# Normalisation factors on GpSimd's queue, and pooled work placed behind the latest operand split

## The chip, the cores and the metric

The kernel runs on one core of one Trainium2 chip. The metric is the device time of one execution in microseconds (us). Engines are named as the profile names them: PE (TensorE), DVE (VectorE), ACT (ScalarE), POOL (GpSimd) and SP (SyncE). SP computes nothing; it issues DMAs.

## The reference

The reference is a trunk with one layer, a pooling mixer with a SiLU gate, between two RMS normalisations. The input `x` is 1 x 4096 x 1024 in float32. A mixer of a second kind stands in the file but isn't reached with one layer.

```python
def rms_norm(x, w):
    return x * lax.rsqrt(jnp.mean(x * x, axis=-1, keepdims=True) + 1e-6) * w

def pool_mixer(h, in_w, group_w, group_b, scale, out_w):
    u, gate = jnp.split(h @ in_w, 2, axis=-1)              # in_w: 1024 x 2048
    ug = u.reshape(b, s, 4, 256)
    pooled = jnp.stack([trailing_mean(ug[:, :, g], w)      # w = 2, 4, 8, 16 tokens
                        for g, w in enumerate((2, 4, 8, 16))], axis=2) - ug
    mixed = jnp.einsum('bsgc,gcd->bsgd', pooled, group_w) + group_b
    return (mixed.reshape(b, s, 1024) * scale * jax.nn.silu(gate)) @ out_w

def reference(x, norm_w, ...):
    h = x + pool_mixer(rms_norm(x, norm_w[0]), ...)
    return rms_norm(h, final_norm_w)
```

## The kernel before, in words

**Arithmetic.** Every float32 product is made of three matmuls. An operand is split into a rounded high part and the residual, its low part; the products high x high, high x low and low x high are added up in a bank of PSUM. `split` (the function at lines 153 to 156) makes both parts of a tile: ACT copies the source into the high part (the copy stands at line 151), then DVE subtracts that high part from the source and writes the low part (line 145). `latest_split[0]` holds the DVE instruction of the latest split.

**Products.** Each matrix product is cut into two by two blocks and done by a scheme of seven products, P1 to P7, in place of eight. Sums and differences of the blocks are formed on DVE (`add` at L142, `sub` at L145) before they are split, and the results are added up in PSUM and, in part, by DVE and ACT when banks are evicted.

**Steps.** The program is a list of steps, one product each. The 4096 tokens are four blocks b = 0 to 3 of 1024. First come 28 "a" steps, seven for each block (the first half of the channels and their gate), then 28 "b" steps, again seven for each block (the second half), all in the order P1, P2, P6, P7, P5, P4, P3, 48 matmuls each. Behind them stand 56 "o" steps, the output projection: eight blocks o0 to o7 of 512 tokens, in the order P1, P7, P6, P2, P5, P4, P3, 24 matmuls each. All of them are issued in `mm3` (L570).

**The main loop (L1171 to L1235).** For step n it records, in this order: loads for steps ahead; at "a" steps the factors of the next block (below); sums and differences for step n + 2 (`form`); the splits of a step ahead; pooled work that is due (`pool_due(n)`, L1210); the step itself (`run(n)`: its matmuls, then the evictions of its banks); at "a" steps a second call of `pool_due` (L1225). Each engine then works through its own instructions in the order in which they stand in its queue, and waits there where an instruction's inputs or its output buffer aren't ready. `tc.issue_after(instruction)` puts what is recorded inside it behind that instruction in the queue of an engine; it adds no work. All DMAs issued by SP stand in one queue too, with the waits in front of them.

**Evictions.** In "a" and "b" steps ACT copies P1's banks into other banks (L151, bank to bank), applies SiLU after P2, and copies or DVE adds (L142) the others. In "o" steps DVE adds the banks of most products onto the rows of `x` (L892).

**Pooled work.** `pool` (L617 to L669) takes the evicted tiles of one half of a block. For each of two channel groups it copies the last 16 columns of the half before into the tile's halo and saves its own last columns (ACT, tile `tails`), builds the trailing sums by one to four shifted additions (DVE, L142; for a window of two one subtraction, L145), scales them and subtracts the tile (DVE, L655), adds the bias and multiplies by the gate (DVE, L660, twice), and stores the result to DRAM (`yd`, SP, L664). It gives back the buffers (`vt`, `st`) at its end. `pool_later` (L974) notes the work after steps P4 and P3, due after a wait of some steps: 0 and 1 for "a"; 1 and 2 for "b", in the last block 2 and 5.

**Factors.** Each block's rows need a factor, 1 / sqrt(mean of squares + eps). For blocks 1 to 3 the factors come in two halves while the "a" steps of the block before run: rows of `x` are loaded (SP, L400), squared and summed (ACT, L407), the root is taken (ACT L192, DVE L196) and refined (POOL, L193 and L206 to L211). Then `store_rs` (L420) stores the half's 512 factors to DRAM, 2 KB, and `load_rstd` (L452) loads them back spread over all 128 partitions, 256 KB, once the store has landed. DVE multiplies the input tiles by them (L148) before they are formed and split. For block 0 the factors are spread by matmuls in `spread_rs`. Inputs for the coming steps (`xt`, L485) and the saved operands (`sd`) are loaded through SP as well; L476 saves operands through ACT's queue, a few of the first through GpSimd's.

**The last block.** During block 3's "b" steps the weights of the output projection (`wod`, loaded at L330) are brought in and split; the tiles `w` in the profile are theirs.

Of the kernel before, what the change touches and what calls it, by code (L numbers as in the profile page):

```python
# [15 lines left out]
P = 128  # L16
# [44 lines left out]
def kernel(  # L61
# [32 lines left out]
    nc = tc.nc  # L94
# [33 lines left out]
    def take(pattern="p (a b) -> p a b", pool=None, **sizes):  # L128
        sizes = sizes or {"a": 2}
        if pool is None:  # L130
            spare = len(vt.free) > keep[0] or not st.free
            pool = vt if spare and vt.age() < st.age() else st
        return pool.take(lambda t: t[:, 0:D].rearrange(pattern, **sizes))

    def take_v():
        return vt.take(lambda t: t.rearrange("p (a b) -> p a b", a=2))

    def give(ap):
        next(p for p in (st, vt, early, early5) if id(ap) in p.used).give(ap)

    def add(dst, a, b):
        nc.vector.tensor_tensor(out=dst, in0=a, in1=b, op=ALU.add)  # L142

    def sub(dst, a, b):
        return nc.vector.tensor_tensor(out=dst, in0=a, in1=b, op=ALU.subtract)  # L145

    def mul(dst, a, b):
        nc.vector.tensor_tensor(out=dst, in0=a, in1=b, op=ALU.mult)  # L148

    def copy(dst, src, func=AF.Copy):  # L150
        return nc.scalar.activation(dst, src, func)  # L151

    def split(dst, src):

        copy(dst[:, 0], src)
        latest_split[0] = sub(dst[:, 1], src, dst[:, 0].bitcast(F32)).ins

    latest_split = [None]

    colt = const.tile([P, 24], F32, name="colt")  # L160
    norm_c = [colt[:, k : k + 1] for k in range(NK)]
# [19 lines left out]
    rd = [[dram.tile([1, H], F32, name=f"rd{b}_{t}") for t in range(2)] for b in range(NB)]  # L181
# [125 lines left out]
    def split_wb(i):  # L307
        for h in range(2):
            (u,) = parts.pop((i, h)).values()
            if i == P1:  # L310
                split_scaled(w[i][h], u, pair(norm_c, h, 0))
            elif i == P2:
                split_scaled(w[i][h], u, pair(norm_c, h, 1))
            else:
                split(w[i][h], u)
            if i != P6:
                give(u)
# [9 lines left out]
    def load_w(src, i):  # L327
        for h in range(2):
            u = take()
            nc.sync.dma_start(out=u, in_=src[i][h])  # L330
            split(w[i][h], u)
            give(u)
# [25 lines left out]
    def split_early(place, u, pattern, **sizes):  # L358

        flat = place.rearrange("p s a b -> p s (a b)")  # L360
        split(flat, u.rearrange("p a b -> p (a b)" if len(u.shape) == 3 else "p k t c -> p (k t c)"))
        return [flat[:, j].rearrange(pattern, **sizes) for j in range(2)]
# [49 lines left out]
    def stats(b, half):  # L412
        ms = small.tile([P, 4], F32, tag="ms", name=f"ms{b}_{half}")
        tmp = small.tile([P, 4], F32, tag="tmp", name=f"tmp{b}_{half}")
        rs = small.tile([P, 4], F32, tag="rs", name=f"rs{b}_{half}")
        rsqrt(rs, tmp, ms, sums[b, half], b == 0)
        return rs

    def store_rs(b, half, rs):
        nc.sync.dma_start(out=rd[b][half][0].rearrange("(p j) -> p j", j=4), in_=rs)  # L420

    spread_done = [None]

# [23 lines left out]
    rstd = {}  # L447

    def load_rstd(b, half):
        if half == 0:  # L450
            rstd[b] = take()
        nc.sync.dma_start(out=rstd[b][:, half], in_=rd[b][half][0].partition_broadcast(P))  # L452

    def normalize(b, half, u):
        mul(u, u, rstd[b][:, half].unsqueeze(1).to_broadcast([P, 2, H]))
# [161 lines left out]
    def pool(b, q, half, vs, sgs):  # L617

        first = b == 0 and half == 1
        last = b == NB - 1 and half == 0  # L620
        end = HIST + H
        for g in range(2):
            grp = 2 * q + g
            win = 2 << grp
            v, sg = vs[g], sgs[g]
            if first:
                nc.vector.memset(v[:, :, 0:HIST], 0.0)
                if win == 2:
                    copy(v[:, :, HIST - 1 : HIST], v[:, :, HIST : HIST + 1])
            else:  # L630
                copy(v[:, :, 0:HIST], tails[:, g])
            if not last:
                copy(tails[:, g], v[:, :, H:])
            s = take_v()
            at = HIST
            if win == 2:
                sub(s[:, :, at:], v[:, :, at - 1 : end - 1], v[:, :, at:])
            else:
                lo = HIST - (win - 2)
                add(s[:, :, lo:], v[:, :, lo:end], v[:, :, lo - 1 : end - 1])  # L640
                n = 2
                while n < win:
                    lo = HIST - (win - 2 * n)
                    size = end - lo
                    a = at - HIST + lo
                    add(s[:, :, a - n : a - n + size], s[:, :, a : a + size],
                        s[:, :, a - n : a - n + size])
                    at -= n
                    n *= 2
                if first:  # L650
                    mul(
                        s[:, :, at : at + HIST], s[:, :, at : at + HIST],
                        invt[:, grp].unsqueeze(1).to_broadcast([P, 2, HIST]),
                    )
                nc.vector.scalar_tensor_tensor(  # L655
                    out=s[:, :, at : at + H], in0=s[:, :, at : at + H], scalar=1.0 / win,
                    in1=v[:, :, HIST:], op0=ALU.mult, op1=ALU.subtract,
                )
            for j in range(2):
                nc.vector.scalar_tensor_tensor(  # L660
                    out=sg[:, j], in0=s[:, j, at : at + H], scalar=bias_c[2 * grp + j],
                    in1=sg[:, j], op0=ALU.add, op1=ALU.mult,
                )
            nc.sync.dma_start(  # L664
                out=yd[2 * b + 1 - half][:, 2 * grp : 2 * grp + 2, :], in_=sg
            )
            give(v)
            give(s)
            give(sg)  # L669
# [302 lines left out]
    pending = []  # L972
# [11 lines left out]
        pending.append((n + wait, args))  # L984

    def pool_due(n):
        while pending and pending[0][0] <= n:
            pool(*pending.pop(0)[1])


    warm = nc.const_aps.tensor(1.0, [P, H], mybir.dt.bfloat16)
# [42 lines left out]
    with tc.high_priority():  # L1034
        rs = stats(0, 0)
# [43 lines left out]
    with tc.high_priority():  # L1079
        rs = stats(0, 1)  # L1080
# [90 lines left out]
    for n in range(2, len(steps)):  # L1171
        kind, b, i = steps[n]
# [3 lines left out]
        if ahead:  # L1176
            rows, squares = row_plan(b)
            for half, rs in scales.items():
                store_rs(b + 1, half, rs)
                load_rstd(b + 1, half)  # L1180
            scales.clear()
            for j in squares.get(i, ()):
                with tc.issue_after(evicted[0]):
                    square_row(b + 1, j // 4, j % 4)
                if j % 4 == 3:
                    scales[j // 4] = stats(b + 1, j // 4)
            for j in rows.get(i, ()):
                load_row(b + 1, j // 4, j % 4, early if b == 0 and i == P6 else None)
# [18 lines left out]
        if kind == "a" and b == 0:  # L1207
            with tc.issue_after(latest_split[0]):
                rest_of_first(n)
        pool_due(n)  # L1210
        since = n - (NB - 1) * len(ORDER_IN) - 2
        if 0 <= since < len(ORDER_IN):
# [9 lines left out]
        if kind in ("a", "b"):  # L1222
            pool_later(n)
            if kind == "a":
                pool_due(n)  # L1225
            if kind == "b" and b == NB - 1:
                load_w(wod, i)
            if kind == "b" and b in (1, 2) and i == P5:
                make_wo(b - 1)
            if kind == "b" and b == NB - 1 and i == P3:  # L1230
                f = take("p (a b) -> p a b", a=2)
                nc.sync.dma_start(
                    out=f.rearrange("p a b -> p (a b)"), in_=final_w.partition_broadcast(P)
                )
                fw.append(f)  # L1235
# [52 lines left out]
```

## Time and profile before

| | |
|---|---|
| median of 3 runs | 922.96 us (920.47 to 925.06) |
| profiled execution | 926.72 us |
| its span in the profile | 924.9 us, mean granted TensorE clock 0.995 |
| PE busy | 907.7 us, 98% of the span |
| DVE busy | 729.1 us, 79% |
| ACT busy | 449.4 us, 49% |
| POOL busy | 48.9 us, 5% |
| DMA | 177.01 MB, 191 GB/s in the mean |

Busy times are sums over an engine's instructions in one profiled execution. The span runs from the first to the last instruction of the profile; the device time of the same execution is 1.8 us longer. In rows of the timeline the first number is the start in us from the beginning of the span, the second the length; "x2" means that two alike instructions are told as one row, and brackets give the engine's idle time just before and what ended it. In rows of busy time by stretches, each engine's busy time is followed by its instructions in parentheses. Rows of waits give us in total, times, and the longest. Lines "L420" are lines of the kernel before.

### The profile page before, as it was taken

To read this page: it belongs to the slowest core of one execution; us is meant where nothing else is said; L and a number is where in the kernel's file an instruction comes from. 1 tells how busy PE (TensorE), PEld (TensorE's weight loads), DVE (VectorE), ACT (ScalarE), POOL (GpSimd) and SP (SyncE) were. 2 spreads that over 40 slices of the span, in tenths; PEclk is the share of its full clock that TensorE was granted. 3 is DMA by queue.
4 is the path that set the end of the run, shared out by engine and by line. 5 is a ranking of instruction groups with operands and counts; after the bars stand their busy time and mean duration, and the time that the engine had idled before them with its cause. 6 is when DMAs were issued, how large, how long until landed. Compare 5 with 4: busy or idle time off the path is not lost.

```text
span 924.9 us, 11163 instructions
## 1 busy us (share of the span) xinstructions
PE 907.7 (98%) x4212; PEld 791.0 (86%) x4212; DVE 729.1 (79%) x807; ACT 449.4 (49%) x685; POOL 48.9 (5%) x118
## 2 busy tenths in 40 slices
PE   9999989999999999999999999999999999999997
PEld 7888878888878888888888888888888888888886
DVE  3897992895698898597499399799997677677676
ACT  6868547347345655345343544653324424334333
POOL 0022100000000000000000000000201001001010
PEclk9999999999999999999999999999999999999999
DMA  9976766576756636115703563756567446365122
GB/s 344 402 305 202 276 227 173 182 258 229 251 225 226 210 113 228 46 46 187 290 23 122 198 227 114 259 155 199 188 224 233 137 176 228 112 207 199 51 92 91
DMA packets 67573, 177.01 MB, mean 191 GB/s; under 512 B 6720, under 2 KB 24512, under 8 KB 67520
## 3 DMA queue, kind: packets, MB, share of 16 engines
q1 hardware_dynamic: 61616, 156.37, 49.0%
q10 hardware_dynamic: 4176, 13.65, 3.8%
q0 software_dynamic: 1728, 6.29, 1.8%
q8 instruction: 33, 0.54, 0.2%
q14 instruction: 20, 0.16, 0.1%
HBM read 115.45 MB, written 60.83 MB: 191 GB/s over the span
## 4 chain that ended last, share of the span: by engine, by line
PE 58%; DVE 24%; DMA 10%; ACT 4%; issue 3%; POOL 1%; SPq 0%; DVEq 0%; ACTq 0%; POOLq 0%
PE bank L570 56%; DVE vt L142 6%; DVE op L145 5%; DVE st L145 3%; PE bank L373 2%; DVE st L148 2%; DVE vt L655 1%; DMA st<-in_out_w 1%; DMA rd<-rs 1%; DVE st L142 1%; DMA wod<-st 1%; DVE vt L660 1%; DMA st<-rd 1%; ACT op L151 1%; DMA st<-wvd 1%
## 5 line engine op out<-in xcount | busy, mean ns | idle before, releaser
L570 PE MATMUL bank<-op,w 128*128 128x512 f32 x2688 | 586.0, 381 | 8.4 <-DVE op L145 5.5
L570 PEld LDWEIGHTS bank<-op,w 128*128 128x128 f32 x2688 | 509.7, 190 | 83.9 <-DVE op L145 7.6
L570 PE MATMUL bank<-w,op 128*128 128x512 f32 (+1 forms) x1356 | 290.3, 377 | 0.0
L570 PEld LDWEIGHTS bank<-w,op 128*128 128x128 f32 x1356 | 254.6, 189 | 35.8
L151 ACT ACTIVATE op<-st 128x1024 fp32r<-128x1024 f32 x126 | 131.7, 1051 | 140.2 <-PE bank L570 116.0
L145 DVE TENSOR_TENSOR op<-st,op 128x1024 fp32r<-128x1024 f32 x126 | 153.3, 1224 | 54.2 <-ACT op L151 54.2
L142 DVE TENSOR_TENSOR vt<-vt 128x1028 f32<-128x1028 f32 (+6 forms) x72 | 88.1, 1239 | 0.1
L151 ACT ACTIVATE vt<-bank 128x512 f32<-128x512 f32 x102 | 58.1, 593 | 31.3 <-PE bank L570 31.0
L151 ACT ACTIVATE op<-vt 128x1024 fp32r<-128x1024 f32 x40 | 42.2, 1054 | 58.5 <-PE bank L570 58.3
L145 DVE TENSOR_TENSOR st<-st,st 128x1024 f32<-128x1024 f32 x38 | 46.2, 1225 | 23.9 <-DMA st<-wvd 9.1
L892 DVE TENSOR_TENSOR st<-bank,st 128x512 f32<-128x512 f32 x60 | 41.2, 692 | 26.4 <-PE bank L570 26.2
L145 DVE TENSOR_TENSOR op<-vt,op 128x1024 fp32r<-128x1024 f32 x40 | 48.9, 1224 | 7.6 <-ACT op L151 7.4
L193 POOL TENSOR_SCALAR oms<-oss 128x2 f32<-128x2 f32 x14 | 11.7, 839 | 613.9 <-ACT st L781 609.5
L151 ACT ACTIVATE bank<-bank 128x512 f32<-128x512 f32 x48 | 27.8, 582 | 29.0 <-PE bank L570 22.0
L142 DVE TENSOR_TENSOR vt<-bank,vt 128x512 f32<-128x512 f32 (+1 forms) x55 | 36.0, 680 | 0.0
L892 DVE TENSOR_TENSOR vt<-bank,vt 128x512 f32<-128x512 f32 (+1 forms) x37 | 24.8, 674 | 11.7 <-PE bank L570 11.4
L145 DVE TENSOR_TENSOR w<-st,w 128x1024 fp32r<-128x1024 f32 x20 | 24.2, 1223 | 7.0 <-ACT w L151 7.0
L655 DVE SCALAR_TENSOR_TENSOR vt<-vt,vt 128x1024 f32<-128x1024 f32 x24 | 29.5, 1229 | 0.0
L148 DVE TENSOR_TENSOR st<-st,st 128x1024 f32<-128x1024 f32 (+1 forms) x19 | 21.7, 1165 | 9.8 <-DMA st<-rd 9.1
L660 DVE SCALAR_TENSOR_TENSOR vt<-vt,colt,vt 128x512 f32<-128x512 f32 x38 | 27.0, 755 | 0.0
L151 ACT ACTIVATE w<-st 128x1024 fp32r<-128x1024 f32 x20 | 20.9, 1057 | 12.5 <-PE bank L570 10.8
L151 ACT ACTIVATE vt<-vt 128x1024 f32<-128x1024 f32 (+1 forms) x12 | 11.8, 987 | 30.8 <-DVE vt L142 30.8
(121 smaller groups left out, 517.1 us busy)
## 6 DMA issues: line engine op xcount, KB each, us to landing
st<-in_x SPq DMA_DIRECT2D x33, 512.0 KB, 5.3
st<-sd SPq DMA_DIRECT2D x29, 512.0 KB, 4.8
st<-in_xt SPq DMA_DIRECT2D x25, 512.0 KB, 6.7
vt<-in_x SPq DMA_DIRECT2D x24, 512.0 KB, 5.1
sd<-st ACTq DMA_DIRECT2D x19, 512.0 KB, 4.4
yd<-vt SPq DMA_DIRECT2D x19, 512.0 KB, 3.0
st<-yd SPq DMA_DIRECT2D x19, 512.0 KB, 4.7
out<-st SPq DMA_DIRECT2D x17, 512.0 KB, 4.6
```

Source lines behind the costliest of these rows:

```text
L142: nc.vector.tensor_tensor(out=dst, in0=a, in1=b, op=ALU.add)
L145: return nc.vector.tensor_tensor(out=dst, in0=a, in1=b, op=ALU.subtract)
L148: nc.vector.tensor_tensor(out=dst, in0=a, in1=b, op=ALU.mult)
L151: return nc.scalar.activation(dst, src, func)
L193: nc.gpsimd.tensor_scalar(out=ms, in0=ss, scalar1=1.0 / D, scalar2=EPS, op0=ALU.mult, op1=ALU.add)
L373: latest[0] = nc.tensor.matmul(ps2[kk][:, j * 256 : (j + 1) * 256], a[:, kk, 2 * j + t, :], b[:, 2 * j + t, :], start=t + m == 0, stop=t = ...
L570: latest[0] = nc.tensor.matmul(ps, a, b, start=start and n == 0, stop=stop and n == 2, skip_group_check=True).ins
L655: nc.vector.scalar_tensor_tensor(out=s[:, :, at : at + H], in0=s[:, :, at : at + H], scalar=1.0 / win, in1=v[:, :, HIST:], op0=ALU.mult, o ...
L660: nc.vector.scalar_tensor_tensor(out=sg[:, j], in0=s[:, j, at : at + H], scalar=bias_c[2 * grp + j], in1=sg[:, j], op0=ALU.add, op1=ALU.mult,)
L892: partial["added"] = nc.vector.tensor_tensor(out=dst, in0=src, in1=dst, op=ALU.add).ins
```

## The change

`split` now also keeps its ACT instruction, as `latest_split[1]`. `store_rs` and `load_rstd` issue their DMAs from GpSimd's queue in place of SP's: six stores of 2 KB and six loads of 256 KB, for two halves of blocks 1 to 3. `pool_due` records all pooled work behind the latest split, behind its DVE instruction on DVE and behind its ACT instruction on ACT. The same instructions are issued as before; their order on DVE and ACT, and by way of the buffers the order of some DMAs on SP and of four matmuls on PE near the first output steps, is another one.

```diff
     def split(dst, src):
 
-        copy(dst[:, 0], src)
+        latest_split[1] = copy(dst[:, 0], src).ins
         latest_split[0] = sub(dst[:, 1], src, dst[:, 0].bitcast(F32)).ins
 
-    latest_split = [None]
+    latest_split = [None, None]
...
     def store_rs(b, half, rs):
-        nc.sync.dma_start(out=rd[b][half][0].rearrange("(p j) -> p j", j=4), in_=rs)
+        nc.gpsimd.dma_start(out=rd[b][half][0].rearrange("(p j) -> p j", j=4), in_=rs)
...
         if half == 0:
             rstd[b] = take()
-        nc.sync.dma_start(out=rstd[b][:, half], in_=rd[b][half][0].partition_broadcast(P))
+        nc.gpsimd.dma_start(out=rstd[b][:, half], in_=rd[b][half][0].partition_broadcast(P))
...
     def pool_due(n):
-        while pending and pending[0][0] <= n:
-            pool(*pending.pop(0)[1])
+        with tc.issue_after(latest_split[0]), tc.issue_after(latest_split[1]):
+            while pending and pending[0][0] <= n:
+                pool(*pending.pop(0)[1])
```

## The prediction

> **What bounds the kernel now.** I read the page's busy shares first, then busy time in 40 us stretches, then the waits, and last the timeline around each loss. PE is the bound, with DVE close behind:
>
> ```profile
> PE 907.7 (98%) x4212; PEld 791.0 (86%) x4212; DVE 729.1 (79%) x807; ACT 449.4 (49%) x685; POOL 48.9 (5%) x118
> ```
>
> The stretches show where the missing time lies (matmuls behind PE busy, then DVE, the granted clock last but two):
>
> ```profile
> core 0: us, PE busy (x) PEld busy (x) DVE busy (x) ACT busy (x) POOL busy (x), PEclk, DMA share, GB/s
> ...
> 100.00:140.00 40.00, 37.53 (x167) 32.21 (x166) 39.69 (x41) 19.17 (x30) 0.00 (x0) 0.96 0.65 224
> 140.00:180.00 40.00, 40.00 (x187) 35.03 (x186) 19.60 (x22) 22.95 (x38) 3.83 (x10) 1.00 0.62 193
> 180.00:220.00 40.00, 39.58 (x184) 34.32 (x183) 35.81 (x36) 20.67 (x35) 0.00 (x0) 1.00 0.64 230
> ...
> 260.00:300.00 40.00, 37.91 (x167) 32.28 (x166) 36.13 (x36) 19.41 (x32) 0.00 (x0) 0.96 0.68 250
> ...
> 540.00:580.00 40.00, 38.46 (x179) 33.36 (x178) 40.00 (x41) 19.19 (x29) 0.00 (x0) 1.00 0.38 135
> ...
> 620.00:660.00 40.00, 40.00 (x187) 35.03 (x186) 39.97 (x43) 12.62 (x16) 0.00 (x0) 1.00 0.49 160
> ```
>
> A full stretch touches 187 matmuls (two cut by its edges), so one costs about 40 / 186 = 0.215 us. Four stretches fall short, by 20, 3, 20 and 8 matmuls: 4.3 + 0.65 + 4.3 + 1.7 = 10.95 us. The first three are the starts of blocks 1, 2 and 3 (I call them transitions 1, 2, 3), the fourth is block 3's second "b" step. Beyond these only the head of the program loses, which the change does not reach. So 10.95 us is all that can be won. Each loss in the timeline (start, length, last the wait before it):
>
> ```profile
> 121.06 2.35 DVE L145 TENSOR_TENSOR op<-st,op 128x1024 fp32r<-128x1024 f32 x2
> ...
> 122.33 1.98 PE L570 MATMUL bank<-op,w 128*128 128x512 f32 x5 [2.47 <-DVE op L145]
> ...
> 272.37 2.26 PE L570 MATMUL bank<-op,w 128*128 128x512 f32 x6 [2.02 <-DVE op L145]
> ...
> 568.98 0.57 ACT L151 ACTIVATE bank<-bank 128x512 f32<-128x512 f32 x1
> ...
> 569.61 1.56 PE L570 MATMUL bank<-op,w 128*128 128x512 f32 x6 [1.54 <-ACT bank L151]
> ```
>
> Twice PE waits for the low part of P2's operand (the DVE half of a split), once for ACT's copy of a bank. After the first two the clock drops:
>
> ```profile
> 122.90:126.30 3.40, 3.40 (x10) 2.64 (x9) 3.40 (x5) 0.00 (x0) 0.00 (x0) 0.50 0.76 272
> 126.30:129.70 3.40, 3.40 (x17) 3.00 (x16) 3.40 (x5) 0.41 (x1) 0.00 (x0) 1.00 0.72 280
> ```
>
> 10 matmuls where 17 or 18 fit: some 7.5 x 0.215 = 1.6 us on top of the wait. The wait of 1.54 us brought no drop (clock 1.00 in that stretch), so the point lies between 1.54 and 2.02 us of idle.
>
> **The change, part by part.** *The factors' queue.* Six 2 KB stores (L420) and six 256 KB loads (L452) leave SP's queue for GpSimd's; none is added. What each side has cost:
>
> ```profile
> 80.84 0.33 SPq L420 DMA_DIRECT2D rd<-rs  x1
> 81.26 0.38 SPq L485 DMA_DIRECT2D st<-in_xt  x1
> 82.30 0.33 SPq L452 DMA_DIRECT2D vt<-rd  x1
> 82.72 0.38 SPq L400 DMA_DIRECT2D st<-in_x  x1
> ...
> 89.52 1.06 ACT L407 ACTIVATE st<-st 128x1024 f32<-128x1024 f32 x1 [2.60 <-DMA st<-in_x]
> ...
> 93.13 0.18 DVE L196 RECIPROCAL rs<-tmp 128x4 f32<-128x4 f32 x1 [1.99 <-ACT tmp L192]
> ```
>
> Transition 1: SP's queue is in order. The xt load at 81.26 and the in_x load at 82.72 stand behind the store, which waits for GpSimd's statistics until 80.84, and the load at 82.30, which waits for that store to land. Freed, both can leave up to about 2 us sooner. ACT's square then loses some of its 2.60 us wait, and DVE some of the 1.99 us in front of the reciprocal. From there DVE runs without a hole to the split at 121.06 (39.69 of 40 us busy), so what is won there arrives at PE. I take 1.8 of at most 1.99 (the memsets of the pooled buffers, now among this work, are some 0.2), below at nothing. PE's wait becomes 2.47 - 1.8 = 0.7, under the clock's point: the loss goes from 4.3 to about 0.9; with nothing won it is 4.5.
>
> ```profile
> 166.47 3.96 DMA rd<-rs
> 170.49 5.63 DMA st<-rd
> ...
> 239.67 8.01 DMA rd<-rs
> 247.70 3.49 DMA st<-rd
> ...
> 234.07 1.28 SPq L485 DMA_DIRECT2D st<-in_xt  x3
> 235.45 1.93 SPq L485 DMA_DIRECT2D vt<-in_xt  x3
> ...
> 251.28 1.23 DVE L148 TENSOR_TENSOR st<-st,st 128x1024 f32<-128x1024 f32 x1 [5.53 <-DMA st<-rd]
> ...
> DMA to landing us min/median/max: 1.4/4.2/8.0
> ...
> L476 POOL DMA_DIRECT2D sd<-st x3: 531/531/719, 50.6 to 59.9; - x3
> ...
> 50.00:60.00 10.00, 9.42 (x44) 7.94 (x43) 10.00 (x10) 6.99 (x9) 6.05 (x12) 1.00 0.79 306
> ```
>
> Transition 3 (the chain of waits): the 2 KB store took 8.01 us, behind six 512 KB loads issued from 234.07 on in the same ring; the shortest of its kind (L420's landings, the row with three numbers) took 1.4, the median 4.2. In a ring of its own I take 3 to 4, so 4 to 5 us less, and DVE's wait of 5.53 at 251.28 falls to about 1. That covers PE's 2.02 with 2 us over: 4.3 becomes 0.3. Transition 2: store 3.96 and load 5.63; the load against the 3.49 above can win about 2. PE lost 0.65 there and the pooled work is moved behind the normalisation as well: 0.2 left, 0.65 if nothing is won.
>
> The price is GpSimd issuing: 531 ns (L476's row) against 0.33 us for SP's, 0.2 more for each of the two DMAs in the chain. GpSimd is idle otherwise, and those DMAs were issued from 50.6 to 59.9 us, while DVE was busy 10.00 of 10 us (last row), so 0.4 us in all, against more than 2 won.
>
> [...]
>
> [...]
>
> *Pooled work behind the latest split.* No instruction is added; the order on DVE and ACT changes in most of the program. In the starts of blocks this puts P1's and P2's splits ahead of pooled operations of 1.2 us, which helps. In block 3's "b" steps:
>
> ```profile
> 566.95 0.23 ACT L151 ACTIVATE vt<-tails 128x32 f32<-128x32 f32 x1 [4.74 <-DVE vt L142]
> ...
> 576.62 1.06 ACT L151 ACTIVATE w<-vt 128x1024 fp32r<-128x1024 f32 x1 [3.52 <-DMA vt<-wod]
> ...
> 584.28 2.36 DVE L145 TENSOR_TENSOR op<-st,op 128x1024 fp32r<-128x1024 f32 x2
> ```
>
> ACT's copy of the bank (568.98) stood behind the halo copy of the pooled work at 566.95, which waited 4.74 us for DVE. With pooled copies behind the split the bank goes first: 1.7 becomes 0.1. But DVE is busy 40.00 of 40 us there, and the same DVE work still stands ahead of the split at 584.28 for P7 (some 78 matmuls of P2 and P6 from 569.61 on put P7 at 586.5, and at 584.8 once P2 no longer stalls). Its first part ended at 585.45. So DVE is 0.6 late if all else stays. The pooled operations now come as one run of ten, so the buffer that the load of w2 (the copy at 576.62, which waited 3.52 for it) goes into comes free several operations later; I add 0.6. P7: 1.2, bounds 0 and, if the load's 3.5 us shows in full, 4.
>
> At the first output steps (o0) the order moves DVE's eviction of P7's bank (L892) four places ahead, in front of pooled operations; P5's evictions, which P3 needs, have as many instructions ahead of them as before:
>
> ```profile
> 627.99 12.25 PE L570 MATMUL bank<-w,op 128*128 128x512 f32 x56
> ...
> 634.60 1.23 DVE L145 TENSOR_TENSOR st<-st,st 128x1024 f32<-128x1024 f32 x1
> ...
> 652.81 8.37 PE L570 MATMUL bank<-w,op 128*128 128x512 f32 x38
> ...
> 656.81 0.71 DVE L892 TENSOR_TENSOR st<-bank,st 128x512 f32<-128x512 f32 x1
> ...
> 658.54 0.71 DVE L892 TENSOR_TENSOR st<-bank,st 128x512 f32<-128x512 f32 x1
> ```
>
> Place for place DVE's queue reached the new point at 634.60, and P7 of o0 ends at 638.35 (o0 starts at 627.99; two steps of 24 matmuls, 5.18 us each). DVE, which had no hole (39.97 of 40), then waits up to 3.75 us with the pooled run behind it. P5's first eviction ended at 657.5, and P3 starts at 659.07 (six steps from 627.99; the row at 652.81 shows no gap). Moved by 3.75 the eviction ends at 661.3, 2.2 late; four matmuls of the next group now stand ahead of P3 and give 0.86 back. The loss is 1.3 to 2.2, I take 1.6; nothing if the wait is not there.
>
> **The sum.** Losses after: 0.9 + 0.2 + 0.3 + 0.1 + 1.2 + 1.6 = 4.3, against 10.95: 6.65 us less. I round the gain to 6.5 for the memsets and GpSimd's issues. The profiled execution took 926.72 (span 924.9), 0.4% above the median of 922.96; I take the gain off both: 920.2 for an execution like that, 916.5 for the median.
>
> **The rivals.** First, transition 1 is not cured: the loads freed in SP's queue meet other limits, as buffers that come free late. Against it stands only the position of the xt load. Loss 4.5 instead of 0.9: gain 2.9, 920.1.
>
> Second, the two new waits pass the clock's point: P7's and P3's idle time reach 2.2 each, and each brings 1.6. Losses 0.9 + 0.2 + 0.3 + 0.1 + 3.8 + 3.8 = 9.1: 921.1. P3's bound of 2.2 speaks for it.
>
> Third, slower. ACT's side of the new order holds DVE back:
>
> ```profile
> ACT op L151 <- PE bank L570: 174.3, 68, 6.9
> ```
>
> ACT's split waits for PE to free its operand buffer, 68 times, 2.6 us in the mean and 6.9 at most. The halo copies now stand behind it, DVE's pooled adds wait for them, and the evictions and splits that PE needs stand behind the adds. Where DVE has no spare time (540 to 660) one such mean wait lands on PE at P7 and again at P3: 3.8 and 4.2, with the clock's 1.6 each. With transition 1 uncured: 4.5 + 0.6 + 3.8 + 4.2 + 3.2 = 16.3, 5.4 more than now: 928.3; with longer waits up to 8.6 more. It decides once the two gaps pass 2 us each and transition 1 stays; DVE's 21% idle over the program speaks against it, its full stretches for it.
>
> Fourth, the factors come no sooner: GpSimd's DMAs take the longer of what rows show (4.2 and 5.6). Then transitions 1 to 3 stay: 4.5 + 0.65 + 4.3 + 0.1 + 1.2 + 1.6 = 12.4, 924.4: the queue move does not do what it says.
>
> **How the numbers follow.** My forecast 0.45, the first rival 0.17, the second 0.13, the third 0.18, the fourth 0.07. A measurement of this kernel can tell about 0.5%, 4.6 us, from no change. Faster by more: 0.40 of the forecast's 0.45 and 0.05 of the first two, 0.45. Slower by more: the third with its worse half and a little of the fourth, 0.19. The rest, 0.36, lies within. The range goes from 912 (all 10.95 us won) to 927, which leaves out most of the third rival.
>
> **What would show it.** Right: the granted clock stays 1.00 in the stretches of 100 to 140 and 260 to 300; no wait of PE over 1 us before 300; the store of the factors for block 3 lands within 4 us; PE waits once for DVE near 585 and once for L892 near 660. Wrong: PE waits for L145 at transition 1 by over 2 us; landings of the factors over 5 us; half-clock stretches after 540; or PE gaps in the "b" steps of blocks 0 to 2, where I expect none.

## The result: slower by half a per cent, and the profile after

The changed kernel took 927.66 us in the median of 11 runs (925.25 to 930.25), the kernel before 922.26 (919.62 to 925.06): 1.0052 times as long, with a 95% interval of 1.0036 to 1.0068. The forecast was 916.5, the range 912 to 927, so the sign was wrong and the time lies just outside.

The two profiled executions do not show this: 925.75 us after, 926.72 before. Read alone, they would tell of a small gain. The changed kernel's lies at the low end of its runs, and that of the kernel before lies above all of its eleven. What they do show is where the losses moved. Busy time by stretch in the changed kernel, in the columns of before:

```profile
100.00:140.00 40.00, 39.26 (x183) 34.05 (x182) 38.82 (x39) 19.92 (x33) 0.57 (x1) 1.00 0.66 226
...
180.00:220.00 40.00, 38.19 (x178) 33.10 (x177) 33.80 (x33) 21.44 (x36) 0.19 (x1) 1.00 0.66 237
...
260.00:300.00 40.00, 38.14 (x178) 33.07 (x177) 34.53 (x36) 21.49 (x35) 0.00 (x0) 1.00 0.71 260
...
540.00:580.00 40.00, 40.00 (x187) 35.04 (x186) 40.00 (x40) 20.53 (x34) 0.00 (x0) 1.00 0.35 119
580.00:620.00 40.00, 37.90 (x176) 32.89 (x175) 30.70 (x31) 21.56 (x27) 0.00 (x0) 1.00 0.65 211
620.00:660.00 40.00, 38.40 (x178) 33.30 (x178) 39.31 (x41) 10.92 (x20) 0.00 (x0) 1.00 0.43 144
660.00:700.00 40.00, 39.66 (x184) 34.28 (x183) 35.79 (x42) 19.94 (x30) 5.65 (x15) 1.00 0.72 242
```

Short of 187 by 4, 9, 9, 11, 9 and 3 matmuls: 45 x 0.215 = 9.7 us, where the first profile of before lost 10.95. Block 1's start fell from 4.3 to 0.9, block 3's from 4.3 to 1.9; block 2's rose from 0.65 to 1.9. Two losses are new: 2.4 us behind 580 (block 3's P7) and 1.9 behind 620 (o0's P3). The last, 0.65 behind 660, is new as well, at o1's P6. PE's waits in the timeline, without the short one at o1:

```profile
120.24 3.94 PE L570 MATMUL bank<-op,w 128*128 128x512 f32 x17 [0.74 <-DVE op L145]
...
194.83 2.43 PE L570 MATMUL bank<-op,w 128*128 128x512 f32 x10 [1.81 <-DVE op L145]
...
269.65 2.64 PE L570 MATMUL bank<-op,w 128*128 128x512 f32 x11 [1.86 <-DVE op L145]
...
582.81 1.56 PE L570 MATMUL bank<-op,w 128*128 128x512 f32 x6 [2.10 <-DVE op L145]
...
657.85 1.35 PE L570 MATMUL bank<-w,op 128*128 128x512 f32 x5 [1.60 <-DVE st L892]
```

### The profile page after: what moved, and what is told of

The parts are those of the page before. It is cut to its first block, busy times and chain, and to the rows that moved or that the text cites. A ratio compares the mean times of both kernels' runs of the same rounds, so it can differ in the third digit from the quotient of the medians.

```text
span 924.0 us, 11202 instructions
## 1 busy us (share of the span) xinstructions
PE 905.8 (98%) x4212; PEld 788.6 (85%) x4212; DVE 729.9 (79%) x807; ACT 448.7 (49%) x685; POOL 52.6 (6%) x130
## 4 chain that ended last, share of the span: by engine, by line
PE 79%; DVE 10%; ACT 4%; DMA 4%; issue 2%; SPq 0%; POOL 0%; DVEq 0%; ACTq 0%; POOLq 0%
PE bank L570 79%; DVE vt L142 2%; DVE op L145 2%; DMA early<-in_wut 2%; DMA st<-in_x 2%; DVE st L148 1%; ACT early L407 1%; DVE st L145 1%; ACT op L151 1%; DVE st L892 1%; DVE vt L655 1%; ACT w L151 1%; DVE vt L660 1%; PE bank L373 0%; DVE w L145 0%
## 5 line engine op out<-in xcount | busy, mean ns | idle before, releaser
L142 DVE TENSOR_TENSOR vt<-vt 128x1024 f32<-128x1024 f32 (+6 forms) x72 | 85.9, 1232 | 0.1
L193 POOL TENSOR_SCALAR oms<-oss 128x2 f32<-128x2 f32 x14 | 9.7, 689 | 609.4 <-ACT st L781 604.9
L142 DVE TENSOR_TENSOR vt<-bank,vt 128x512 f32<-128x512 f32 (+1 forms) x55 | 35.9, 679 | 2.6 <-PE bank L570 2.6
L151 ACT ACTIVATE w<-st 128x1024 fp32r<-128x1024 f32 x20 | 20.9, 1055 | 18.3 <-PE bank L570 11.3
L148 DVE TENSOR_TENSOR st<-st,st 128x1024 f32<-128x1024 f32 (+1 forms) x19 | 21.7, 1164 | 8.9 <-DMA st<-rd 8.2
L785 DVE SCALAR_TENSOR_TENSOR st<-st,ors,st 128x1024 f32<-128x1024 f32 x17 | 21.4, 1281 | 6.5 <-POOL ors L211 6.5
```

The source lines that it names most:

```text
L193: nc.gpsimd.tensor_scalar(out=ms, in0=ss, scalar1=1.0 / D, scalar2=EPS, op0=ALU.mult, op1=ALU.add)
L785: nc.vector.scalar_tensor_tensor(out=us[j], in0=us[j], scalar=rs[:, j : j + 1], in1=fw[0], op0=ALU.mult, op1=ALU.mult,)
```

## Experiments: which part, which call, which mechanism

**Second executions of both kernels.** First question: is the first profile of before typical? Both kernels were run again, unchanged.

> The kernel before, unchanged, for a second profiled execution. Theory A (the profiled execution of before that the forecast was built on was dearer than its usual one, because both half-clock stretches at the starts of blocks 1 and 3 fell into it): the profile ends near 920 to 922 us of span and shows the clock at 1.00 in the stretches 100:140 and 260:300, with waits of PE there all the same; losses at the transitions sum to 7 to 8 us in place of 10.95. Theory B (that execution is typical, and the changed kernel loses in places that its own profile does not show): the span is 923 to 925 and the two half-clock stretches are there again.

> The changed kernel once more, for a second profiled execution of it: its first (925.75 us) lies at the lower end of its eleven times (925.25 to 930.25). Theory A (half-clock stretches come and go with the execution): this one shows one or two stretches at a clock of about 0.5 after the waits at block 2, block 3, block 3's P7 or o0's P3, which are 2 to 2.5 us in all executions, each 1.6 to 1.8 us. Theory B: the waits themselves differ by 1 us and more between executions.

Measured: before 921.97 us (profiled execution 920.02), after 928.92 (929.22), against 922.65 for the runs of before beside them; the second ratio is 1.0068 (1.0045 to 1.0091). The second profile of before:

```profile
100.00:140.00 40.00, 37.62 (x175) 32.63 (x174) 39.63 (x41) 19.68 (x31) 0.00 (x0) 1.00 0.65 224
...
180.00:220.00 40.00, 40.00 (x186) 34.76 (x185) 34.30 (x34) 22.10 (x37) 0.19 (x1) 1.00 0.66 237
...
260.00:300.00 40.00, 38.62 (x180) 33.50 (x179) 33.48 (x35) 21.06 (x36) 0.00 (x0) 1.00 0.72 256
...
540.00:580.00 40.00, 40.00 (x187) 35.04 (x186) 40.00 (x41) 22.81 (x34) 0.00 (x0) 1.00 0.39 134
```

Only 12, 1 and 7 matmuls are missing, 4.3 us in place of 10.95, and less than the 7 to 8 that theory A expected. The clock stays at 1.00, and the wait in block 3's second b step is not there at all. In the second profile of after, 580 to 620 holds 167 matmuls at a clock of 0.96 where the first held 176 at 1.00. So the clock's drops come and go, as theory A said; but some waits do too, as theory B said: in the two profiles of after PE waits 0.74 and 2.37 us at block 1, while the new waits recur within some 0.2 us (PE idle 1.81 and 1.86 us in 180 to 220, 2.10 and 2.32 in 580 to 620). Time less losses agrees between these three executions: 926.72 - 10.95 = 915.8, 920.02 - 4.3 = 915.7, 925.75 - 9.7 = 916.0. The losses are the whole difference between them, and an execution of before can win 4.3 us at most when it has lost only that.

**Each half of the change alone.** `queue_only` makes only the two edits from `nc.sync` to `nc.gpsimd`; `order_only` makes all others.

> Only the factors' twelve DMAs go to GpSimd's queue; pooled work stands as before. Theory A1 (the queue move helps, the order of the pooled work costs): PE's wait at the start of block 1 falls from 2.5 to about 0.7 us, at block 3 it stays near 2 or falls, the wait of 1.5 us in block 3's second b step stays, no wait at its P7 and none at o0's P3; 1 to 4 us faster than before. Theory B1 (GpSimd's DMAs cost, their loads land in 5.8 us where SP's took 4.7): waits at the starts of blocks 2 and 3 grow, and the time is 1 to 4 us slower than before.

> Only pooled work is put behind the latest split; the factors stay in SP's queue. Theory A1: the wait at block 1 stays near 2.5 us, the wait in block 3's second b step goes, and about 2.4 us at its P7, 1.9 at o0's P3 and 0.6 in o1's P6 come instead; with the clock dropping after some of them 4 to 9 us slower than before. Theory B1 (the order is harmless and the queue costs): within 2 us of before.

Measured: the queue alone 920.82 us, 0.9985 (0.9968 to 1.0001); in another set 920.88, 0.9984 (0.9968 to 0.9999). The order alone 932.20 us, 1.0096 (1.0069 to 1.0123). The order costs some 9 us and the queue wins 1.6 to 1.8 without it, 3.3 to 4.5 with it. Part of the latter lies at block 3's start, where the profile of `order_only` lacks 17 matmuls and the first of after 9. The expectation for the second set of the queue alone:

> Only the factors' DMAs on GpSimd's queue, once more, for a second profile and a firmer time. If the gain is real: 1 to 3 us faster than before; PE's wait at block 1 under 2.5, at block 2 under 0.5, at block 3 about 2. If it was chance: within 1 us of before.

Theory A1 holds in its direction, with a gain that is hardly clear of noise: one of the two intervals includes 1. PE's wait at block 1 fell less than it said, to 1.98 and 1.53 us in the two profiles, and the wait in block 3's second b step, which was to stay, is in neither. The rows of `order_only` show the new waits at block 2, at P7 and at o0's P3:

```profile
198.10 2.21 PE L570 MATMUL bank<-op,w 128*128 128x512 f32 x9 [1.81 <-DVE op L145]
...
587.46 2.93 PE L570 MATMUL bank<-op,w 128*128 128x512 f32 x6 [2.14 <-DVE op L145]
...
664.14 2.21 PE L570 MATMUL bank<-w,op 128*128 128x512 f32 x9 [1.60 <-DVE st L892]
```

**Which calls, and which engine.** In `order_a` and `order_b` the edges apply on one condition; `dve_edge` keeps the edge to the DVE instruction alone, `after_sooner` shortens the dues.

```diff
+        held_back = steps[n][0] == "a"          # order_b: != "a"
-        with tc.issue_after(latest_split[0]), tc.issue_after(latest_split[1]):
+        with (
+            tc.issue_after(latest_split[0]) if held_back else nullcontext(),
+            tc.issue_after(latest_split[1]) if held_back else nullcontext(),
+        ):
...
+        with tc.issue_after(latest_split[0]):    # dve_edge
...
-            wait = 0 if kind == "a" else 1 if b < NB - 1 else 2
+            wait = 0 if kind == "a" else 0 if b < NB - 1 else 1    # after_sooner
-            wait = 1 if kind == "a" else 2 if b < NB - 1 else 5
+            wait = 1 if kind == "a" else 1 if b < NB - 1 else 4
```

> The factors stay in SP's queue; pooled work is put behind the latest split only when it is called from a steps. Theory L: the waits at the starts of blocks 2 and 3 are 2 us and more each, because pooled operations that stood in DVE's wait for the factors now come after it; nothing new in b and o steps; 2 to 5 us slower than before. Rival Q': the a steps are harmless and all of the loss is in b and o steps: within 1 us of before.

> The factors stay in SP's queue; pooled work is put behind the latest split only when it is called from b and o steps. Theory L (lost idle time: DVE's free time of about 5 us before block 3's b steps, which pooled work used to fill, is left empty, and DVE is then full for 45 us, so that P7 comes late): the start of block 2 costs 0.2 to 0.7 us as before, block 3's P7 2.4 to 4.3, o0's P3 1.9, o1's P6 0.6; DVE is idle about 5 us shortly before block 3's b steps; 4 to 6 us slower than before. Rival Q (the pooled work is harmful because it comes as a run in front of evictions and weight loads, wherever DVE was before): the same waits, but no idle time of DVE ahead of them.

> The factors stay in SP's queue; pooled work is put behind the latest split on DVE only (DVE's order is that of the version with both edges, ACT's is not). Theory L: all new waits stay (block 3's P7 2.4 or more, o0's P3 1.9, o1's P6 0.6, blocks 2 and 3 about 2 each): 6 to 10 us slower than before. Theory ACT (halo copies behind ACT's operand copies, which wait for PE, hold DVE back: the third rival of the prediction): most of the new waits go; within 3 us of before.

> The changed kernel with pooled work of b steps due one step sooner (waits 0 and 1, in the last block 1 and 4, in place of 1 and 2, 2 and 5), so that the split it stands behind is an earlier one. Theory L: DVE's idle time before block 3's b steps is filled, P7's wait of 2.4 to 4.3 us falls under 1, and so does P3's of 1.9 at o0; 4 to 6 us faster than the changed kernel, about the time of before. Rival Q: the runs stand as before in front of evictions and loads, and the waits stay within 1 us of what they are.

Measured: a steps alone 926.33 us, 1.0041 (1.0022 to 1.0060); b and o steps alone 926.74, 1.0056 (1.0035 to 1.0077). Together that is the 1.0096 of the whole order. With the edge on DVE alone 932.56, 1.0101 (1.0068 to 1.0135): DVE's order alone gives the whole loss, so the prediction's third rival, in which ACT's halo copies hold DVE back, falls. `after_sooner` took 929.63, 1.0077 (1.0050 to 1.0103), no gain on the changed kernel, where theory L had expected 4 to 6 us. The cure did not come about: DVE's idle time ahead of block 3 was still there (busy 15.1 of the 20 us), and the wait moved from P7 to P6, where PE now waited 3.24 us. It decides nothing between the theories, since it did not change what theory L blames.

**One call alone, and all but that one.** Theory L says that DVE loses free time ahead of a stretch in which it is full. The changed kernel shows the hole, a wait for saved operands that pooled work used to fill, and the split for P7:

```profile
535.05 1.23 DVE L145 TENSOR_TENSOR st<-st,st 128x1024 f32<-128x1024 f32 x1 [3.99 <-DMA st<-sd]
...
581.54 2.36 DVE L145 TENSOR_TENSOR op<-st,op 128x1024 fp32r<-128x1024 f32 x2
```

`edge_one` is the kernel before with the edge on a single call; `b_but_one` has it on all b calls but that one.

```diff
+            args = pending.pop(0)[1]
+            held_back = args[:3] == (2, 1, 1)    # b_but_one: args[1] == 1 and args[:3] != (2, 1, 1)
```

> The kernel before, with a single call of the pooled work put behind the latest split: that for the tiles of block 2's b step P4, which ran before in the stretch 25 to 5 us ahead of block 3's b steps. Theory L: DVE is idle for 5 to 6 us in that stretch, is then full for 40 us, and block 3's P7 waits 2.4 to 4 us for DVE's split; no wait at o0; 2.5 to 5 us slower than before. Rival Q (runs of pooled work in front of later evictions and weight loads): no effect from one call that lies 30 us ahead, within 1.5 us of before.

> Pooled work of all b steps behind the latest split, but for that one call, which stands as before; factors in SP's queue. Theory L: DVE is busy 19 to 20 of the 20 us ahead of block 3's b steps, the wait at block 3's P7 falls from 2.4 to 4.3 to under 1; o0's P3 keeps 1.9 and o1's P6 0.6: 1 to 3 us slower than before. Rival Q: P7's wait stays above 2, 3 to 6 us slower.

Measured: `edge_one` 928.40 us, 1.0062 (1.0037 to 1.0086), 6.0 us slower and so more than expected; `b_but_one` 926.19, 1.0034 (1.0018 to 1.0050), 0.7 us more than expected. Stretches of 20 and 36 us, from 25 us ahead of block 3's b steps to its P7, for before (second profile), `edge_one` and `b_but_one`:

```profile
523.80:543.80 20.00, 20.00 (x94) 17.52 (x93) 19.97 (x23) 6.32 (x11) 0.00 (x0) 1.00 0.61 228
543.80:579.80 36.00, 36.00 (x168) 31.53 (x167) 36.00 (x35) 20.67 (x31) 0.00 (x0) 1.00 0.42 148
```

```profile
526.00:546.00 20.00, 20.00 (x94) 17.54 (x93) 14.80 (x18) 4.78 (x7) 0.00 (x0) 1.00 0.63 240
546.00:582.00 36.00, 36.00 (x168) 31.58 (x167) 36.00 (x35) 18.75 (x32) 0.00 (x0) 1.00 0.35 118
...
538.64 2.45 DVE L145 TENSOR_TENSOR st<-st,st 128x1024 f32<-128x1024 f32 x2 [5.20 <-DMA st<-sd]
...
585.22 2.34 DVE L145 TENSOR_TENSOR op<-st,op 128x1024 fp32r<-128x1024 f32 x2
...
586.49 3.98 PE L570 MATMUL bank<-op,w 128*128 128x512 f32 x10 [4.05 <-DVE op L145]
```

```profile
528.50:548.50 20.00, 20.00 (x94) 17.56 (x93) 19.54 (x22) 6.14 (x8) 0.00 (x0) 1.00 0.54 202
548.50:584.50 36.00, 36.00 (x169) 31.56 (x168) 32.79 (x32) 20.12 (x31) 0.00 (x0) 1.00 0.39 135
```

This is the clearest reading of the study. With the one call held back DVE is busy 14.80 us of 20 instead of 19.97: 5.2 us of free time are lost. In the next 36 us DVE has none to make up for it (36.00 of 36.00), and PE waits 4.05 us at P7. With that call as before and all other b calls held back, DVE is busy 19.54 of 20 and P7 does not wait; o0's P3 still does. PE is full in both stretches of all three: the harm is done 40 us before it shows. Rival Q, which expected no effect from this one call, falls.

P7 waits 4.05 us with one call held back and 2.10 with all of them. In both, DVE works without a hole from the end of its wait for saved operands to the split for P7, and about as long: 581.54 - 535.05 = 46.5 us in the changed kernel, 585.22 - 538.64 = 46.6 in `edge_one`. PE comes to P7 at 580.71 and at 582.44 (the start of its row less its idle time), so DVE's wait ended 45.7 us ahead of that in the one and 43.8 in the other. That accounts for the difference: the later the saved operands land, the longer P7 waits. What made them late in `edge_one` is not traced.

**The last block's calls.** `edge_last` holds back `args[:2] == (3, 1)` alone.

> The kernel before, with only the last block's two calls of pooled work (after its b steps P4 and P3) behind the latest split. As the prediction had it for the output steps: no wait at block 3's P7, DVE idle 2 to 4 us between 625 and 640 us, 1.9 us lost at o0's P3 and 0.6 at o1's P6; 1.5 to 3.5 us slower than before. Rival (these waits follow from DVE's lag at block 3's P7): no wait at o0 and o1, within 1 us of before.

Measured: 924.94 us, 1.0032 (1.0019 to 1.0045). P7 does not wait, o0's P3 does, and the wait at o1's P6 did not come. DVE's stretches in `edge_last`, then in before (second profile), and P3's row in `edge_last`:

```profile
603.00:623.00 20.00, 20.00 (x94) 17.53 (x94) 16.66 (x17) 11.80 (x18) 0.00 (x0) 1.00 0.45 157
623.00:643.00 20.00, 20.00 (x95) 17.53 (x94) 19.14 (x22) 5.76 (x9) 0.00 (x0) 1.00 0.48 153
...
617.07 1.22 DVE L145 TENSOR_TENSOR w<-st,w 128x1024 fp32r<-128x1024 f32 x1 [2.20 <-ACT w L151]
...
655.14 3.10 PE L570 MATMUL bank<-w,op 128*128 128x512 f32 x9 [1.85 <-DVE st L892]
```

```profile
603.00:623.00 20.00, 20.00 (x94) 17.53 (x93) 19.93 (x21) 11.31 (x14) 0.00 (x0) 1.00 0.46 157
623.00:643.00 20.00, 20.00 (x94) 17.50 (x94) 20.00 (x22) 5.68 (x7) 0.00 (x0) 1.00 0.63 202
```

Again free time is lost, 3.3 us in the first 20 us and 0.9 in the next. DVE waits for ACT's copies of weights (2.20 us at 617.07) where pooled additions stood before. Most of that comes before o0 begins, at 621 us, and not at the eviction that the prediction named, nor between 625 and 640 us, where the expectation put it.

**The a steps, and what is left of the order.** `edge_a1` holds back `args[:3] == (1, 0, 1)`, block 1's call after P4; `edge_a_half0` the a calls after P3; `after_rest` is the changed kernel without the edge on any call blamed above.

> The kernel before, with a single call of the pooled work put behind the latest split: that for block 1's a step P4, whose operations stood ahead of and around DVE's wait for block 2's factors. Theory L: one of its operations of 1.1 us no longer runs in that wait but after it, and the start of block 2 loses 1.1 to 2.1 us where it lost 0.2 to 0.7; block 3's start and all later steps as before; 0.5 to 2.5 us slower. Rival (the waits of 2 us at blocks 2 and 3 come from the calls after P3): the start of block 2 as before, within 0.5 us.

> The kernel before, with only the a steps' calls after P3 behind the latest split (those after P4 as before). Theory L: nothing of DVE's waiting time is given up, so the starts of blocks 2 and 3 lose what they lose in the kernel before (0.2 to 0.7, and 1.6 to 4); within 1.5 us of before. Rival: 2 us lost at block 2.

> The changed kernel without the edges on the calls that theory L blames: those after P4 in a steps, that for block 2's b step P4, and both of block 3's b steps. The factors stay in GpSimd's queue and the other calls keep their edges. Theory L: no wait over 1 us after the start of block 3, the time of the version with the queue move alone, 919 to 922 us. Rival (the harm is spread over all of the calls): 923 us or more.

Measured: `edge_a1` 923.55 us, 1.0020 (1.0003 to 1.0036); `edge_a_half0` 922.69, 1.0020 (1.0005 to 1.0036); `after_rest` 920.33, 0.9990 (0.9976 to 1.0004). Block 2's start in `edge_a1`, then in `edge_a_half0`:

```profile
180.00:220.00 40.00, 39.36 (x183) 34.16 (x182) 34.21 (x34) 21.04 (x35) 0.19 (x1) 1.00 0.64 237
```

```profile
180.00:220.00 40.00, 40.00 (x188) 35.01 (x187) 33.76 (x33) 22.02 (x38) 0.19 (x1) 1.00 0.66 237
```

The call after P4 makes block 2's start lose 4 matmuls, 0.9 us, just under the 1.1 to 2.1 expected; the calls after P3 make it lose nothing. The changed kernel loses 1.9 us there. DVE's rows tell the rest: its wait for the last factors (L148), the operation that the edge moves behind that wait (L142) and the split for P2, in before (first profile), `edge_a1` and after:

```profile
171.33 1.22 DVE L142 TENSOR_TENSOR vt<-vt 128x1024 f32<-128x1024 f32 x1
...
176.14 1.23 DVE L148 TENSOR_TENSOR st<-st,st 128x1024 f32<-128x1024 f32 x1 [3.60 <-DMA st<-rd]
...
195.94 2.36 DVE L145 TENSOR_TENSOR op<-st,op 128x1024 fp32r<-128x1024 f32 x2
```

```profile
173.39 1.23 DVE L148 TENSOR_TENSOR st<-st,st 128x1024 f32<-128x1024 f32 x1 [2.81 <-DMA st<-rd]
...
175.73 1.22 DVE L142 TENSOR_TENSOR vt<-vt 128x1024 f32<-128x1024 f32 x1
...
194.33 2.36 DVE L145 TENSOR_TENSOR op<-st,op 128x1024 fp32r<-128x1024 f32 x2
...
195.61 4.58 PE L570 MATMUL bank<-op,w 128*128 128x512 f32 x20 [0.64 <-DVE op L145]
```

```profile
172.61 1.23 DVE L148 TENSOR_TENSOR st<-st,st 128x1024 f32<-128x1024 f32 x1 [3.99 <-DMA st<-rd]
...
174.95 1.22 DVE L142 TENSOR_TENSOR vt<-vt 128x1024 f32<-128x1024 f32 x1
...
193.56 2.36 DVE L145 TENSOR_TENSOR op<-st,op 128x1024 fp32r<-128x1024 f32 x2
```

From the factors to the split it is 195.94 - 176.14 = 19.8 us before and 20.9 in both others: the edge costs one operation, 1.1 us, and the one call gives all of it. The rest is when the factors land. PE comes to P2 at 194.97 in `edge_a1` and at 193.02 in after, so they were there 21.6 us ahead of it in the one and 20.4 in the other; this 1.2 us is the difference of PE's waits, 0.64 and 1.81. What lets them land later in after is not traced. In time the two versions cannot be told apart, and `edge_a_half0` is slower by 0.05 to 0.36% without a place for it in its profile. `after_rest` is level with the queue move alone and, at its median, 5 us below the changed kernel's lowest run: the rest of the order costs nothing that shows, and brings nothing. So the fastest version is the queue move, by itself (0.9985 and 0.9984 of before) or with the rest of the order (0.9990); of the three intervals only one stays below 1, and only just.

## Why the prediction was wrong

**The ceiling.** All that can be won was put at 10.95 us. That was one execution's bill: its two clock drops (3.2 us) and the wait in block 3's second b step (1.7) were missing in the next one, which lost 4.3. The gain was taken off the median, though the execution stood 4 us above it; the text noted the 0.4% and did not draw the conclusion. By the 915.8 us that the three executions above leave without losses, the median of before loses some 6.5 us and that of the changed kernel some 11.9, as an estimate. The sum had 10.95 and 4.3. The change was forecast as 6.65 us faster and measured as 5.4 slower. Of these 12 us the ceiling explains some 4.5, and the losses after, in the terms below, the other 7.6; they gave the wrong sign.

**The queue.** At block 1 the step held in the first profile of after: ACT's wait of 2.60 us for the load fell to 0.75 and PE's loss to the 0.9 forecast. In the second the wait was 2.53 again, as before, and PE lost 2.6; with the queue alone ACT still waited 2.25 and 1.82 us. In all, the move is worth some 1.7 us by itself. At block 3, 4 to 5 us were to be won by a queue of its own. Issue, wait and landing after:

```profile
236.78 0.57 POOL L420 DMA_DIRECT2D rd<-rs  x1 [0.41 <-POOL rs L211]
242.33 0.57 POOL L452 DMA_DIRECT2D st<-rd  x1 [4.99 <-DMA rd<-rs]
...
247.44 1.23 DVE L148 TENSOR_TENSOR st<-st,st 128x1024 f32<-128x1024 f32 x1 [4.21 <-DMA st<-rd]
```

From the store's issue to DVE's start it is 247.44 - 236.78 = 10.7 us, against 251.28 - 239.67 = 11.6 before. The store was shorter (5.2 us against 8.0), the load longer (5.1 against 3.5); 0.9 was won, not 4 to 5. In the second profiles it is 10.5 after and 10.6 before, so next to nothing. While the pair of the first profile of after was under way, from 236.78 to 247.44, the 16 DMA engines were busy 0.89 of the time (347 GB/s); SP had issued eight 512 KB loads of `xt` from 224.2 to 234.9, which took 4.7 to 9.8 us to land. That this store would land in 3 to 4 us from a queue of its own was the author's estimate, and no run shows it: the load behind it was issued 5.5 us after it in both profiles of after and 6.6 and 6.7 with the queue alone, against 8.0 and 6.8 before. The median landing of the six loads was 4.7 and 4.3 us before, 5.8 and 5.4 after. GpSimd's issue took 0.57 us, where SP's had taken 0.33 and the prediction took 0.53, and the pair as a whole was no longer than from SP.

**Blocks 2 and 3.** The prediction said that the order puts splits ahead of pooled work there, "which helps", and left 0.2 and 0.3 us. The measured losses are 1.9 each in the changed kernel. The direction was wrong: a pooled operation of 1.1 us that ran ahead of DVE's wait for the factors now follows it, and so stands ahead of the split that PE waits for. At block 3 it is the same 1.1 us (268.38 - 247.44 = 20.9 from the factors to the split, against 271.08 - 251.28 = 19.8); PE waited 2.02 and 1.38 us there before, so its 1.86 now is a loss that was not cured rather than a new one.

**P7 and P3.** Both waits came, at the places named: 2.4 and 1.9 us where the sum had 1.2 and 1.6. P7's term was mis-sized because it counted the same DVE work ahead of the split and took DVE's time before it as unchanged. DVE started that work 5 us in arrears, as the single call of `edge_one` shows. For P3 the size was near by luck: the sum put the cause at the eviction of o0's P7, and most of it lies before o0.

**The rivals.** None was the right one. The first describes block 1 in the second profile of after and the fourth block 3, where the factors came hardly sooner; both took P7 and P3 at the forecast's sizes. The second had two new waits of 2 us, in some executions with the clock's drop, but still a gain. The third had the right sign by a mechanism that `dve_edge` refutes. Of the prediction's signs of being right, the waits near 585 and 660 came, and the clock stayed at 1.00 before 300, as it did in the second profile of before too; of those of being wrong, landings over 5 us came in both profiles of after (up to 6.7 and 6.8), a wait over 2 us at block 1 (2.37) and a stretch below the full clock after 540 (0.96 in 580 to 620) in one.

**What stays open.** What sets the time at which the factors of block 2 and the saved operands ahead of block 3 land is not traced: it made 1.2 us of block 2's wait and the difference between 2.10 and 4.05 us at P7. Nor is it shown where the queue move wins all of its 1.7 us.

## What to carry to other kernels

Pooled work that only filled DVE's waits cost nothing here where it stood, and an ordering edge took that away (for one call 5.2 us of DVE's free time, and PE waited 4.05 us): before adding such an edge, list what the engine does in its idle time ahead of every stretch in which it is full, because the lost time was paid at the end of that stretch here, 40 us later. Take the ceiling of a gain from two or three profiled executions, and set each against the median of the runs before using its losses. Try the two halves of a change apart: here one was worth some 0.16% (0.9984, 0.9968 to 0.9999) and the other cost 0.96%.

## What the hardware did that I had not expected

The length of a wait did not decide here whether PE's granted clock dropped. Idle times of PE of 2.38 us (before, second profile) and 2.62 us (`edge_a_half0`) brought no drop (1.00 from 100 to 140 us in both), 2.02 (before, first profile: 0.60 from 272.40 to 275.80) and 1.85 (`edge_last`: 0.68 from 655.00 to 658.60) did. 2.47 us brought one in before (first profile: 0.50 from 122.90 to 126.30, five matmuls in the 1.98 us of the row behind the wait) and none in `order_b` (nine in 2.21 us there). The rows of the second profile of before, of `edge_a_half0` and of `edge_last`:

```profile
122.27 1.99 PE L570 MATMUL bank<-op,w 128*128 128x512 f32 x8 [2.38 <-DVE op L145]
```

```profile
122.12 2.21 PE L570 MATMUL bank<-op,w 128*128 128x512 f32 x9 [2.62 <-DVE op L145]
...
100.00:140.00 40.00, 37.38 (x174) 32.41 (x173) 39.48 (x41) 18.81 (x31) 0.00 (x0) 1.00 0.64 220
```

```profile
643.00:663.00 20.00, 18.14 (x77) 15.29 (x76) 19.90 (x24) 3.35 (x6) 0.19 (x1) 0.91 0.49 169
```

So no point between 1.54 and 2.02 us, as the prediction had it, parts the waits that brought a drop from those that brought none. What does is not shown by these runs.
